# A new start, and one mixing product per unit on GpSimd, in a fused RWKV time-mixing kernel

## The chip, the cores and the metric

The kernel runs on one core of a Trainium2 chip. The metric is the device time of one execution in microseconds. The kernel before takes 228.21 us (median of three runs, 228.16 to 228.28). Five engines work side by side: TensorE (PE in the profile), VectorE (DVE), ScalarE (ACT), GpSimd (POOL) and SyncE (SP, which here only issues transfers). "L152" in a profile line is a line of the kernel whose profile it is; the two kernels have different line numbers.

## The reference, cut to what matters

`x` has the shape (16, 2048, 256), float32. Only two of the three mixed inputs reach the output:

```python
x_prev[:, 1:, :] = x[:, :-1, :]                    # row before, zero at the start
xv = x * time_mix_v + x_prev * (1 - time_mix_v)
xr = x * time_mix_r + x_prev * (1 - time_mix_r)
v = xv @ value_weight
r = xr @ receptance_weight
out = ((1 / (1 + np.exp(-r))) * v) @ output_weight  # float32
```

## The kernel before

The work is cut into 64 *units* of 512 rows, four to each of the 16 batches. A unit is: eight transposes of x on PE into PSUM, a copy of them to `xt` on ACT, a mixed input `mix` on DVE, two projections r and v on PE (eight matmuls of 512 columns), a sigmoid on ACT, the product `z` on DVE, the output projection on PE (eight matmuls of 256 columns), and a copy of it to SBUF on ACT. The mix factor is folded into the weights, so that mixing is a product of `xt` with a per-row constant and a sum with the next column block. Column slot 0 of `xt` is a copy of the last slot, shifted by one (the "wrap copy", once a batch).

```python
def mixing_scale(b, m, lo, hi):          # two products, ko = 0 and 1
    for ko in range(KO):
        nc.vector.tensor_scalar(out=mix[b][:, m, ko, lo:hi], in0=xt[b][:, ko, lo:hi],
            scalar1=c_sb[:, m, ko : ko + 1], scalar2=None, op0=ALU.mult)

def mixing_add(b, m, lo, hi):            # one sum
    nc.vector.tensor_tensor(out=mix[b][:, m, :, lo:hi], in0=mix[b][:, m, :, lo:hi],
        in1=xt[b][:, :, lo + P : hi + P], op=ALU.add)

for g in range(NU):                      # NU = 64
    ps_r = project(g, 0, ...)            # PE
    nc.scalar.activation(out=s_sb, in_=ps_r, func=ACT.Sigmoid)
    ps_v = project(g, 1, ...)            # PE
    # (cut: unit 0)
    took = take_pieces(g + 3, 1 if g > 8 else 2)
    for piece in took: mixing_scale(*piece)
    nc.vector.tensor_tensor(out=z_sb, in0=s_sb, in1=ps_v, op=ALU.mult)
    for piece in took: mixing_add(*piece)
    advance(START_T[g] if g < len(START_T) else g + LOOK)   # transposes of later units
    if z_prev is not None: output(g - 1, z_prev)
    z_prev = z_sb
```

A *piece* is half a batch (1024 columns) for one of the two inputs; in the steady stage one piece is mixed per unit, some units ahead. All PSUM accumulators have one buffer, those of the transposes two.

## Time and profile before

| | before |
|---|---|
| time, median | 228.21 us |
| profiled execution: time, span | 229.34, 227.6 us |
| DVE, PE, ACT, POOL busy | 203.4, 201.8, 185.4, 13.8 us |
| four units (one batch), middle | 12.57 us |
| start of z in units 0, 1, 2, 3, 5, 7 | 15.35, 19.12, 25.45, 30.63, 40.14, 46.26 us |

The busy shares, the chain, the groups and a unit's timeline are shown in the prediction below. What it only tells of is the start, so here it is: the timeline of the kernel before, columns start, duration, engine, line, operation, and in brackets how long the engine had stood idle and for what.

```profile
11.42 1.24 POOL L118 CAST wo_bf<-wo_f 128x512 bf16<-128x512 f32 x1 [7.38 <-DMA wo_f<-in_output_weight_dram]
...
12.61 1.15 POOL L72 DMA_DIRECT2D x_bf<-in_x_dram  x2
...
20.44 0.62 PE L128 MATMUL ps_t<-ident,x_bf 128*128 128x128 bf16 x8 [2.94 <-DMA x_bf<-in_x_dram]
```

GpSimd took the two in program order: it waited 7.38 us for the output weight before a cast, and only after that issued the load of batch 1, whose transposes therefore started at 20.44.

### The profile page before, as it was taken

What the parts mean: (1) busy time and instruction counts of PE and PEld (TensorE: products, weight loads), DVE (VectorE), ACT (ScalarE), POOL (GpSimd) and SP (SyncE); (2) the same over time, 40 slices, a digit from 0 to 9 for tenths busy, and PEclk for the clock granted to TensorE, in tenths of its full rate; (3) what the DMA queues carried; (4) which work ended last, traced back from release to release, by engine and by line L of the source; (5) the groups of instructions that cost most, each with busy time, mean ns of one, the idle gap of its engine ahead of it and who ended that gap; (6) DMA issues with size and microseconds to landing.
All of it is one profiled execution on the core that took longest, in us unless ns stands there. A gap on an engine that the chain in (4) does not pass through costs nothing.

```text
span 227.6 us, 3894 instructions
## 1 busy us (share of the span) xinstructions
PE 201.8 (89%) x1510; PEld 129.8 (57%) x1538; DVE 203.4 (89%) x288; ACT 185.4 (81%) x194; POOL 13.8 (6%) x41
## 2 busy tenths in 40 slices
PE   0294879899999999999999999999999999989881
PEld 0253547566666666665666566666666665655551
DVE  2478299999999999999999999999999999999941
ACT  2185789898989989899989899898989899985671
POOL 5050101000000101010000001010100000000000
PEclk9998899999999999999999999999999999999998
DMA  5969999999999898989999898989897444434364
GB/s 90 217 109 213 215 161 266 229 324 179 351 173 343 164 301 213 251 265 209 327 189 348 160 328 181 279 229 252 268 216 310 187 184 186 187 161 170 148 261 186
DMA packets 9155, 51.38 MB, mean 226 GB/s; under 512 B 1456, under 2 KB 2352, under 8 KB 3376
## 3 DMA queue, kind: packets, MB, share of 16 engines
q0 software_dynamic: 2736, 16.78, 43.9%
q1 hardware_dynamic: 6400, 34.35, 36.9%
q8 instruction: 12, 0.20, 0.3%
q14 instruction: 7, 0.06, 0.1%
HBM read 34.34 MB, written 33.55 MB: 298 GB/s over the span
## 4 chain that ended last, share of the span: by engine, by line
DVE 73%; issue 12%; PE 6%; DMA 3%; POOL 2%; ACT 2%; POOLq 0%; DVEq 0%
DVE mix L161 29%; DVE z_sb L295 29%; DVE mix L152 14%; DMA x_bf<-in_x_dram 3%; PE psum_o L192 2%; PE psum_v L176 2%; PE psum_r L176 1%; ACT xt L134 1%; DVE xt L136 1%; POOL x_bf L80 1%; POOL xt L124 1%; POOL wo_bf L118 1%; PE ps_t L128 0%; ACT o_sb L210 0%; DVE o_sb L207 0%
## 5 line engine op out<-in xcount | busy, mean ns | idle before, releaser
L176 PEld LDWEIGHTS <-w_bf 128*128 128x128 bf16 x512 | 50.3, 99 | 58.3 <-issue 12.4
L295 DVE TENSOR_TENSOR z_sb<-s_sb,psum_v 128x1024 bf16<-128x1024 bf16 x64 | 77.7, 1213 | 5.8 <-ACT s_sb L284 2.9
L161 DVE TENSOR_TENSOR mix<-mix,xt 128x2048 bf16<-128x2048 bf16 (+1 forms) x66 | 77.8, 1186 | 0.0
L134 ACT COPY xt<-ps_t 128x1024 bf16<-128x1024 bf16 x60 | 60.4, 1013 | 19.0 <-PE ps_t L128 18.9
L210 ACT COPY o_sb<-psum_o 128x1024 f32<-128x1024 f32 x63 | 64.2, 1019 | 6.9 <-PE psum_o L192 6.8
L176 PE MATMUL psum_v<-mix,w_bf 128*128 128x512 bf16 x243 | 64.9, 383 | 5.3 <-DVE z_sb L295 4.5
L284 ACT ACTIVATE s_sb<-psum_r 128x1024 bf16<-128x1024 f32 x64 | 66.6, 1041 | 1.4 <-PE psum_r L176 1.4
L192 PE MATMUL psum_o<-wo_bf,z_sb 128*128 128x256 bf16 x512 | 66.6, 273 | 1.1 <-ACT o_sb L210 1.1
L176 PE MATMUL psum_r<-mix,w_bf 128*128 128x512 bf16 x241 | 65.4, 388 | 1.6 <-DVE mix L161 1.2
L152 DVE TENSOR_SCALAR mix<-xt,c_sb 128x1024 bf16<-128x1024 bf16 (+1 forms) x132 | 56.4, 473 | 3.5 <-ACT xt L238 1.8
L192 PEld LDWEIGHTS <-z_sb 128*128 128x128 bf16 x512 | 47.8, 98 | 7.3 <-DVE z_sb L295 1.0
L128 PEld LDWEIGHTS <-x_bf 128*128 128x128 bf16 x480 | 31.4, 98 | 17.2 <-DMA x_bf<-in_x_dram 3.2
L128 PE MATMUL ps_t<-ident,x_bf 128*128 128x128 bf16 x480 | 36.1, 219 | 3.9 <-DMA x_bf<-in_x_dram 2.9
L72 POOL DMA_DIRECT2D x_bf<-in_x_dram x16 | 8.7, 544 | 121.6 <-PE ps_t L128 118.2
L238 ACT COPY xt<-ps_t 128x1024 bf16<-128x1024 bf16 x4 | 4.0, 1014 | 9.2 <-PE ps_t L232 9.2
L232 PE MATMUL ps_t<-ident,x_bf 128*128 128x128 bf16 x32 | 3.1, 265 | 5.7 <-DMA x_bf<-in_x_dram 5.7
L232 PEld LDWEIGHTS <-x_bf 128*128 128x128 bf16 x32 | 2.5, 119 | 6.6 <-DMA x_bf<-in_x_dram 6.2
L136 DVE COPY xt<-xt 128x254 bf16<-128x254 bf16 x15 | 3.3, 220 | 2.0 <-ACT xt L134 2.0
L111 DVE TENSOR_SCALAR w_bf<-w_f,tms 128x256 bf16<-128x256 f32 x4 | 1.2, 351 | 4.1 <-DMA w_f<-in_value_weight_dram 3.5
L124 POOL MEMSET xt<- 128x2 bf16 x15 | 1.7, 111 | 47.1 <-DVE xt L136 47.1
L145 PE MATMUL ps_t<-ident,x_bf 128*128 128x128 bf16 x2 | 0.4, 298 | 3.8 <-DMA x_bf<-in_x_dram 3.8
L100 DVE TENSOR_SCALAR tms<-tm_sb 128x4 f32<-128x4 f32 x1 | 0.2, 169 | 3.5 <-DMA tm_sb<-in_time_mix_v_dram 3.5
(18 smaller groups left out, 8.6 us busy)
## 6 DMA issues: line engine op xcount, KB each, us to landing
out_dram<-o_sb SPq DMA_DIRECT2D x30, 1024.0 KB, 6.5
x_bf<-in_x_dram POOLq DMA_DIRECT2D x15, 1024.0 KB, 10.2
out_dram<-o_sb SPq DMA_DIRECT2D x3, 512.0 KB, 2.8
x_bf<-in_x_dram POOLq DMA_DIRECT2D x2, 256.0 KB, 6.7
out_dram<-o_sb SPq DMA_DIRECT2D x2, 256.0 KB, 2.1
x_bf<-in_x_dram POOLq DMA_DIRECT2D x1, 448.0 KB, 9.4
w_f<-n_receptance_weight_dram SPq DMA_DIRECT2D x1, 256.0 KB, 3.0
w_f<-in_value_weight_dram SPq DMA_DIRECT2D x1, 256.0 KB, 6.6
```

The lines of the kernel that those rows point to most:

```text
L72: nc.gpsimd.dma_start(out=x_bf[b][:, lo:hi, :], in_=src[:, lo:hi, :])
L128: nc.tensor.transpose(out=ps[:, ko, jj * P : (jj + 1) * P], in_=x_bf[b][:, e * UJ + jj, ko * P : (ko + 1) * P], identity=ident,)
L134: nc.scalar.copy(out=xt[b][:, :, c0 : c0 + TU], in_=ps)
L136: nc.vector.tensor_copy(out=xt[b][:, :, 1:P], in_=xt[b][:, :, J * P : (J + 1) * P - 1])
L152: nc.vector.tensor_scalar(out=mix[b][:, m, ko, lo:hi], in0=xt[b][:, ko, lo:hi], scalar1=c_sb[:, m, ko : ko + 1], scalar2=None, op0=ALU.mult,)
L161: nc.vector.tensor_tensor(out=mix[b][:, m, :, lo:hi], in0=mix[b][:, m, :, lo:hi], in1=xt[b][:, :, lo + P : hi + P], op=ALU.add,)
L176: nc.tensor.matmul(out=ps[:, mo, :], lhsT=w_bf[:, m, ko, mo * P : (mo + 1) * P], rhs=mix[b][:, m, ko, e * TU : (e + 1) * TU], start=(ko == 0),
L192: nc.tensor.matmul(out=ps[:, jj, :], lhsT=z[:, ko, jj * P : (jj + 1) * P], rhs=wo_bf[:, ko, :], start=(ko == 0), stop=(ko == KO - 1),)
L210: nc.scalar.copy(out=o_sb[b][:, j0 : j0 + UJ, :], in_=ps)
L232: nc.tensor.transpose(out=ps[:, ko, jj * P : (jj + 1) * P], in_=x_bf[0][:, g * UJ + jj, ko * P : (ko + 1) * P], identity=ident,)
L284: nc.scalar.activation(out=s_sb, in_=ps_r, func=ACT.Sigmoid)
L295: nc.vector.tensor_tensor(out=z_sb, in0=s_sb, in1=ps_v, op=ALU.mult)
```

## The change

Its intent is to fill the pipeline sooner and to take one of DVE's two products per unit away, onto the idle GpSimd. The core of the diff, with cuts:

```diff
-    LOOK = 7
+    LOOK = 8
+    WARM = 34
+    WARM2 = 10
-    xtpool = ... bufs=2
+    xtpool = ... bufs=3
# start: the first unit and the last rows in float32, from SyncE; all of batches 0 and 1
# issued before any GpSimd arithmetic; weights scaled on GpSimd
+    nc.sync.dma_start(out=x_last, in_=rows(0)[:, J - 1, :])
+    nc.sync.dma_start(out=x_unit, in_=rows(0)[:, 0:UJ, :])
+    nc.scalar.dma_start(out=tm_sb[:, 0, :], ...)   # also tm_sb[:, 1, :]
+    nc.sync.dma_start(out=w_f32[:, 0], ...)
+    nc.scalar.dma_start(out=w_f32[:, 1], ...)
+    load(0, UJ, 2 * UJ)
+    load(0, 2 * UJ, J)
+    load(1)
+    for _ in range(WARM):
+        nc.tensor.matmul(out=warm[:, 0, 0:P], lhsT=zeros, rhs=zeros, start=True, stop=True)
-            nc.vector.tensor_scalar(out=w_bf[:, m, ko, :], ..., scalar2=None, op0=ALU.mult)
+            nc.gpsimd.tensor_scalar(out=w_bf[:, m, ko, :], ..., scalar2=1.0, op0=ALU.mult, op1=ALU.mult)
# ... (cut)
+    def scale_pool(piece, after):
+        op = nc.gpsimd.tensor_scalar(out=mix[b][:, m, 1, lo:hi], in0=xt[b][:, 1, lo:hi],
+            scalar1=c_sb[:, m, 1:2], scalar2=1.0, op0=ALU.mult, op1=ALU.mult)
+        if after is not None:
+            tc.add_manual_dep(op.ins, after.ins.name, SYNC, reason="one at a time")
# ... the loop, steady stage (START_POOL = 8)
+            for i in todo:
+                last = scale(pieces[i], (0,) if i in on_pool else (0, 1))
+        advance(START_T[g] if g < len(START_T) else g + LOOK)   # now ahead of v
         ps_v = project(g, 1, ps_v_pool, "psum_v")
         nc.vector.tensor_tensor(out=z_sb, in0=s_sb, in1=ps_v, op=ALU.mult)
+        if g >= START_POOL - 1 and done < len(pieces):
+            scale_pool(pieces[done], last)        # next unit's piece, ko = 1
+        for i in todo:
+            add(pieces[i])
+        wrap_slots()                              # the wrap copy, now a unit before its first reader
```

Batch 0 is mixed in pieces of one unit, later batches in halves; look-ahead of the mixing is eight pieces.

More of the change, by code (lines that the diff above doesn't have):

```diff
@@ L47 @@
     NU = B * UB
-    LOOK = 7
+    HALF = J * P // 2
+    LOOK = 8
+    WARM = 34
+    WARM2 = 10
     consts = ctx.enter_context(tc.tile_pool(name="consts", bufs=1))
     xpool = ctx.enter_context(tc.tile_pool(name="xpool", bufs=3))
-    xtpool = ctx.enter_context(tc.tile_pool(name="xtpool", bufs=2))
+    xtpool = ctx.enter_context(tc.tile_pool(name="xtpool", bufs=3))
     mixpool = ctx.enter_context(tc.tile_pool(name="mixpool", bufs=2))
@@ L61 @@
     ctx.enter_context(tc.manual_schedule())
+    SYNC = mybir.DependencyInfo(mybir.DependencyClass.Sync, mybir.DependencyReason.DATA)
     x_bf = {}
@@ L66 @@
     o_sb = {}
-    def load(b, pieces):
-        x_bf[b] = xpool.tile([P, J, D], BF16, name="x_bf")
-        src = x[b].rearrange("(p j) d -> p j d", p=P)
-        for lo, hi in pieces:
-            nc.gpsimd.dma_start(out=x_bf[b][:, lo:hi, :], in_=src[:, lo:hi, :])
-    ident = consts.tile([P, P], BF16)
-    load(0, [(J - 1, J)])
-    src0 = x[0].rearrange("(p j) d -> p j d", p=P)
-    def load0(lo, hi):
-        nc.gpsimd.dma_start(out=x_bf[0][:, lo:hi, :], in_=src0[:, lo:hi, :])
-    load0(0, 4)
@@ L83, with rows, load @@
-    make_identity(nc, ident)
-    load0(4, 8)
-    load0(8, 15)
+    zeros = consts.tile([P, P], BF16)
+    nc.vector.memset(zeros, 0.0)
+    ident_f = consts.tile([P, P], FP32)
+    make_identity(nc, ident_f)
+    ident = consts.tile([P, P], BF16)
+    nc.vector.tensor_copy(out=ident, in_=ident_f)
+    def rows(b):
+        return x[b].rearrange("(p j) d -> p j d", p=P)
+    def load(b, lo=0, hi=J):
+        if b not in x_bf:
+            x_bf[b] = xpool.tile([P, J, D], BF16, name="x_bf")
+        nc.gpsimd.dma_start(out=x_bf[b][:, lo:hi, :], in_=rows(b)[:, lo:hi, :])
@@ L87 @@
+    x_last = consts.tile([P, D], FP32)
+    x_unit = consts.tile([P, UJ, D], FP32)
     tm_sb = consts.tile([P, 2, KO], FP32)
     w_f32 = consts.tile([P, 2, KO, D], FP32)
-    for m, (tm, w) in enumerate(
-        [(time_mix_r, receptance_weight), (time_mix_v, value_weight)]
-    ):
-        nc.sync.dma_start(out=tm_sb[:, m, :], in_=tm.rearrange("(ko p) -> p ko", p=P))
-    for m, w in enumerate([receptance_weight, value_weight]):
-        nc.sync.dma_start(out=w_f32[:, m], in_=w.rearrange("(ko p) n -> p ko n", p=P))
@@ L95 @@
-    wo_f32 = consts.tile([P, KO, D], FP32)
-    nc.sync.dma_start(out=wo_f32, in_=output_weight.rearrange("(ko p) n -> p ko n", p=P))
+    wo_f32 = consts.tile([P, KO, D], FP32)
+    nc.sync.dma_start(out=x_last, in_=rows(0)[:, J - 1, :])
+    nc.sync.dma_start(out=x_unit, in_=rows(0)[:, 0:UJ, :])
+    nc.scalar.dma_start(out=tm_sb[:, 0, :], in_=time_mix_r.rearrange("(ko p) -> p ko", p=P))
+    nc.scalar.dma_start(out=tm_sb[:, 1, :], in_=time_mix_v.rearrange("(ko p) -> p ko", p=P))
+    nc.sync.dma_start(
+        out=w_f32[:, 0], in_=receptance_weight.rearrange("(ko p) n -> p ko n", p=P)
+    )
@@ new lines @@
+    nc.scalar.dma_start(
+        out=w_f32[:, 1], in_=value_weight.rearrange("(ko p) n -> p ko n", p=P)
+    )
+    nc.sync.dma_start(out=wo_f32, in_=output_weight.rearrange("(ko p) n -> p ko n", p=P))
+    sig0 = consts.tile([P, 1], BF16)
+    nc.scalar.activation(out=sig0, in_=zeros[:, 0:1], func=ACT.Sigmoid)
+    load(0, UJ, 2 * UJ)
+    load(0, 2 * UJ, J)
+    load(1)
+    warm = ps_o_pool.tile([P, UJ, D], FP32, name="psum_o")
+    for _ in range(WARM):
+        nc.tensor.matmul(out=warm[:, 0, 0:P], lhsT=zeros, rhs=zeros, start=True, stop=True)
@@ L98, with new_xt @@
+    def new_xt(b):
+        xt[b] = xtpool.tile([P, KO, (J + 1) * P], BF16, name="xt")
+        (nc.vector if b == 0 else nc.gpsimd).memset(xt[b][:, :, 0:1], 0.0)
+    new_xt(0)
     tms = consts.tile([P, 2, KO], FP32)
@@ L110 @@
         for ko in range(KO):
-            nc.vector.tensor_scalar(
+            nc.gpsimd.tensor_scalar(
                 out=w_bf[:, m, ko, :],
@@ L114 @@
                 scalar1=tms[:, m, ko : ko + 1],
-                scalar2=None,
+                scalar2=1.0,
                 op0=ALU.mult,
+                op1=ALU.mult,
             )
-    nc.gpsimd.tensor_copy(out=wo_bf, in_=wo_f32)
+    nc.gpsimd.tensor_scalar(
+        out=wo_bf, in0=wo_f32, scalar1=1.0, scalar2=1.0, op0=ALU.mult, op1=ALU.mult
+    )
     def transposes(g):
@@ L122, in transposes @@
         if e == 0:
-            xt[b] = xtpool.tile([P, KO, (J + 1) * P], BF16, name="xt")
-            nc.gpsimd.memset(xt[b][:, :, 0:1], 0.0)
+            new_xt(b)
         ps = ps_t_pool.tile([P, KO, TU], BF16, name="ps_t")
@@ L134, in transposes, with first_transposes, scale_act, scale @@
         nc.scalar.copy(out=xt[b][:, :, c0 : c0 + TU], in_=ps)
-        if e == UB - 1 and b > 0:
-            nc.vector.tensor_copy(
-                out=xt[b][:, :, 1:P], in_=xt[b][:, :, J * P : (J + 1) * P - 1]
-            )
-    def first_prev():
-        xt[0] = xtpool.tile([P, KO, (J + 1) * P], BF16, name="xt")
-        nc.vector.memset(xt[0][:, :, 0:1], 0.0)
-        ps = ps_t_pool.tile([P, KO, TU], BF16, name="ps_t")
+        if e == UB - 1:
+            late_copies.append(b)
+    def first_transposes():
+        pl = ps_v_pool.tile([P, KO, TU], FP32, name="psum_v")
         for ko in range(KO):
             nc.tensor.transpose(
-                out=ps[:, ko, 0:P], in_=x_bf[0][:, J - 1, ko * P : (ko + 1) * P], identity=ident
+                out=pl[:, ko, 0:P], in_=x_last[:, ko * P : (ko + 1) * P], identity=ident_f
             )
-        nc.vector.tensor_copy(out=xt[0][:, :, 1:P], in_=ps[:, :, 0 : P - 1])
-    def mixing_scale(b, m, lo, hi):
+        ps = ps_r_pool.tile([P, KO, TU], FP32, name="psum_r")
         for ko in range(KO):
-            nc.vector.tensor_scalar(
+            for jj in range(UJ):
+                nc.tensor.transpose(
+                    out=ps[:, ko, jj * P : (jj + 1) * P],
+                    in_=x_unit[:, jj, ko * P : (ko + 1) * P],
+                    identity=ident_f,
+                )
+        nc.vector.tensor_copy(out=xt[0][:, :, 1:P], in_=pl[:, :, 0 : P - 1])
+        nc.scalar.copy(out=xt[0][:, 0, P : P + TU], in_=ps[:, 0, :])
+        nc.vector.tensor_copy(out=xt[0][:, 1, P : P + TU], in_=ps[:, 1, :])
+    def scale_act(piece):
+        b, m, lo, hi = piece
+        for ko in range(KO):
+            nc.scalar.mul(
+                out=mix[b][:, m, ko, lo:hi], in_=xt[b][:, ko, lo:hi], mul=c_sb[:, m, ko : ko + 1]
+            )
+    def scale(piece, kos=(0, 1)):
+        b, m, lo, hi = piece
+        for ko in kos:
+            last = nc.vector.tensor_scalar(
                 out=mix[b][:, m, ko, lo:hi],
@@ L158, in mixing_scale, with add @@
             )
-    def mixing_add(b, m, lo, hi):
+        return last
+    def scale_pool(piece, after):
+        b, m, lo, hi = piece
+        op = nc.gpsimd.tensor_scalar(
+            out=mix[b][:, m, 1, lo:hi],
+            in0=xt[b][:, 1, lo:hi],
+            scalar1=c_sb[:, m, 1:2],
+            scalar2=1.0,
+            op0=ALU.mult,
+            op1=ALU.mult,
+        )
+        if after is not None:
+            tc.add_manual_dep(op.ins, after.ins.name, SYNC, reason="one at a time")
+    def add(piece):
+        b, m, lo, hi = piece
         nc.vector.tensor_tensor(
@@ L166, in mixing_add @@
         )
-    def new_mix(b):
-        mix[b] = mixpool.tile([P, 2, KO, J * P], BF16, name="mix")
     def project(g, m, pool, name):
@@ L215, in output, with needs, tile_for, per_unit @@
             nc.sync.dma_start(out=dst[:, a : a + 2 * UJ, :], in_=o_sb[b][:, a : a + 2 * UJ, :])
-    def t_unit(g):
-        b, e = divmod(g, UB)
-        if e == 0 and b + 1 < B and b + 1 not in x_bf:
-            load(b + 1, [(0, J)])
-        if g == 0:
-            return
-        transposes(g)
-    load(1, [(0, J)])
-    first_prev()
-    def transposes0(g):
-        ps = ps_t_pool.tile([P, KO, TU], BF16, name="ps_t")
-        for jj in range(UJ):
-            for ko in range(KO):
-                nc.tensor.transpose(
-                    out=ps[:, ko, jj * P : (jj + 1) * P],
-                    in_=x_bf[0][:, g * UJ + jj, ko * P : (ko + 1) * P],
-                    identity=ident,
-                )
-        c0 = (1 + g * UJ) * P
-        nc.scalar.copy(out=xt[0][:, :, c0 : c0 + TU], in_=ps)
-    tnext = 0
+    pieces = [
+        (0, m, u * TU, (u + 1) * TU) for u in range(UB) for m in range(2)
+    ] + [
+        (b, m, q * HALF, (q + 1) * HALF) for b in range(1, B) for q in range(2) for m in range(2)
+    ]
+    def needs(piece):
+        b, m, lo, hi = piece
+        return hi // TU - 1 if b == 0 else UB * b + UB - 1
+    def tile_for(piece):
+        if piece[0] not in mix:
+            mix[piece[0]] = mixpool.tile([P, 2, KO, J * P], BF16, name="mix")
+    def per_unit(g):
+        if g < len(START_MIX):
+            return START_MIX[g]
+        return min(len(pieces), g + 8)
+    START_T = [3, 5, 7, 9, 11]
+    START_MIX = [4, 6, 8, 10, 12]
+    START_POOL = 8
+    late_copies = []
+    def wrap_slots():
+        while late_copies:
+            b = late_copies.pop()
+            if b > 0:
+                nc.vector.tensor_copy(
+                    out=xt[b][:, :, 1:P], in_=xt[b][:, :, J * P : (J + 1) * P - 1]
+                )
+    tnext = 1
     def advance(limit):
@@ L245, in advance @@
             b, e = divmod(tnext, UB)
-            if e == 0 and b + 2 < B:
-                load(b + 2, [(0, J)])
-            if b == 0:
-                transposes0(tnext)
-            else:
-                transposes(tnext)
-            tnext += 1
-    HALF = J * P // 2
-    START_T = [3, 4, 7, 9]
-    pieces = [(h, m) for h in range(2 * B) for m in range(2)]
-    pnext = 2
-    def take_pieces(limit, most):
-        nonlocal pnext
-        took = []
-        while len(took) < most and pnext <= min(limit, len(pieces) - 1):
-            h, m = pieces[pnext]
-            b, q = divmod(h, 2)
-            if tnext <= UB * b + UB - 1:
-                break
-            if b not in mix:
-                mix[b] = mixpool.tile([P, 2, KO, J * P], BF16, name="mix")
-            took.append((b, m, q * HALF, (q + 1) * HALF))
-            pnext += 1
-        return took
-    advance(1)
-    mix[0] = mixpool.tile([P, 2, KO, J * P], BF16, name="mix")
-    for m in range(2):
-        mixing_scale(0, m, 0, TU)
-    for m in range(2):
-        mixing_add(0, m, 0, TU)
+            if e == 1 and b + 2 < B:
+                load(b + 2)
+            transposes(tnext)
+            tnext += 1
+    first_transposes()
+    for piece in pieces[0:2]:
+        tile_for(piece)
+    scale(pieces[0])
+    scale_act(pieces[1])
+    add(pieces[0])
+    add(pieces[1])
+    advance(1)
+    for _ in range(WARM2):
+        nc.tensor.matmul(out=warm[:, 0, 0:P], lhsT=zeros, rhs=zeros, start=True, stop=True)
+    done = 2
+    on_pool = set()
     z_prev = None
     for g in range(NU):
+        todo = list(range(done, per_unit(g)))
+        for i in todo:
+            assert needs(pieces[i]) < tnext, (g, i)
+            tile_for(pieces[i])
+        done = max(done, per_unit(g))
         ps_r = project(g, 0, ps_r_pool, "psum_r")
@@ L284 @@
         nc.scalar.activation(out=s_sb, in_=ps_r, func=ACT.Sigmoid)
-        ps_v = project(g, 1, ps_v_pool, "psum_v")
-        if g == 0:
-            for m in range(2):
-                mixing_scale(0, m, TU, 2 * TU)
-            for m in range(2):
-                mixing_add(0, m, TU, 2 * TU)
-        took = take_pieces(g + 3, 1 if g > 8 else 2)
-        for piece in took:
-            mixing_scale(*piece)
+        last = None
+        if g == 0:
+            for i in todo:
+                scale(pieces[i])
+            for i in todo:
+                add(pieces[i])
+            todo = []
+        elif g < START_POOL:
+            for i in todo[:-1]:
+                scale(pieces[i])
+                add(pieces[i])
+            if todo:
+                last = scale(pieces[todo[-1]])
+        else:
+            for i in todo:
+                last = scale(pieces[i], (0,) if i in on_pool else (0, 1))
+        advance(START_T[g] if g < len(START_T) else g + LOOK)
+        ps_v = project(g, 1, ps_v_pool, "psum_v")
         z_sb = zpool.tile([P, KO, TU], BF16, name="z_sb")
         nc.vector.tensor_tensor(out=z_sb, in0=s_sb, in1=ps_v, op=ALU.mult)
-        for piece in took:
-            mixing_add(*piece)
-        advance(START_T[g] if g < len(START_T) else g + LOOK)
+        if late_copies and done < len(pieces) and pieces[done][0] in late_copies:
+            wrap_slots()
+        if g >= START_POOL - 1 and done < len(pieces):
+            tile_for(pieces[done])
+            assert needs(pieces[done]) < tnext
+            scale_pool(pieces[done], last)
+            on_pool.add(done)
+        if g < START_POOL:
+            todo = todo[-1:]
+        for i in todo:
+            add(pieces[i])
+        wrap_slots()
         if z_prev is not None:
```

## The prediction

> **What bounds the kernel now.** I read first the busy shares, then the chain that ended last, then the groups of instructions, then the timeline of one unit in the middle and of the last units.
>
> ```profile
> PE 201.8 (89%) x1510; PEld 129.8 (57%) x1538; DVE 203.4 (89%) x288; ACT 185.4 (81%) x194; POOL 13.8 (6%) x41
> ...
> DVE 73%; issue 12%; PE 6%; DMA 3%; POOL 2%; ACT 2%; POOLq 0%; DVEq 0%
> ```
>
> Two engines show the same 89%, so busy time doesn't choose between them. The chain does: 73% of the span is DVE, 6% PE. GpSimd (POOL) is idle.
>
> ```profile
> L295 DVE TENSOR_TENSOR z_sb<-s_sb,psum_v 128x1024 bf16<-128x1024 bf16 x64 | 77.7, 1213 | 5.8 <-ACT s_sb L284 2.9
> L161 DVE TENSOR_TENSOR mix<-mix,xt 128x2048 bf16<-128x2048 bf16 (+1 forms) x66 | 77.8, 1186 | 0.0
> ...
> L152 DVE TENSOR_SCALAR mix<-xt,c_sb 128x1024 bf16<-128x1024 bf16 (+1 forms) x132 | 56.4, 473 | 3.5 <-ACT xt L238 1.8
> ```
>
> These three groups are DVE's work in a unit (512 rows): z, one sum, two products. Durations overlap a little at their ends, so I work with start-to-start times ("pitch"), from the timeline of a unit in the middle:
>
> ```profile
> 123.79 0.61 PE L128 MATMUL ps_t<-ident,x_bf 128*128 128x128 bf16 x8
> 123.93 0.88 DVE L152 TENSOR_SCALAR mix<-xt,c_sb 128x1024 bf16<-128x1024 bf16 x2
> ...
> 124.24 1.04 PE L192 MATMUL psum_o<-wo_bf,z_sb 128*128 128x256 bf16 x8
> ...
> 124.72 1.21 DVE L295 TENSOR_TENSOR z_sb<-s_sb,psum_v 128x1024 bf16<-128x1024 bf16 x1
> ...
> 125.85 1.22 DVE L161 TENSOR_TENSOR mix<-mix,xt 128x2048 bf16<-128x2048 bf16 x1
> ...
> 126.99 0.22 DVE L136 COPY xt<-xt 128x254 bf16<-128x254 bf16 x1
> ```
>
> DVE: two products 0.79 (123.93 to 124.72), z 1.13, sum 1.14: 3.06 us. Once per batch of four units a wrap copy adds 0.33 (0.22 plus a short wait). A batch takes 4 x 3.06 + 0.33 = 12.57 us, as the chain has it (its products start at 64.88, 77.45, 90.01), or 3.14 per unit. ACT's three instructions have a pitch of about 0.9 each, some 2.75.
>
> PE is the engine to look at next. In the last units there are no transposes, and PE alone sets the pace:
>
> ```profile
> 215.69 0.81 PE L176 MATMUL psum_r<-mix,w_bf 128*128 128x512 bf16 x3
> ...
> 216.55 1.03 PE L176 MATMUL psum_v<-mix,w_bf 128*128 128x512 bf16 x4
> ...
> 217.41 1.04 PE L192 MATMUL psum_o<-wo_bf,z_sb 128*128 128x256 bf16 x8
> ...
> 218.28 1.03 PE L176 MATMUL psum_r<-mix,w_bf 128*128 128x512 bf16 x4
> ```
>
> From 215.69 to 218.28 is 2.59 us for the two projections and the output. The eight transposes add 0.45 (123.79 to 124.24 above): **3.04 us per unit is what PE needs**, only 0.10 under today's 3.14.
>
> **What the Trainium skill says.** (1) "TensorE: Matmul & The Clock Gate", section "Wait — 56ns, not 53.3ns?": warm matmuls start N / 2.4 GHz + 2.5 ns apart, 55.6 ns for 128 columns, 215.7 for 512. Eight of each, with eight of 256 columns at 109 ns, make 3.04 us: the trace agrees. So 3.04 is a floor, not a schedule. (2) "SBUF — State Buffer", section "Who interferes with whom": a DVE instruction in a two-port mode, or with two SBUF inputs while GpSimd reads SBUF, shares a port with GpSimd, and the second to start waits; one with at most one SBUF input in neither mode doesn't contend. The mixing products and sums are of the first two kinds. z (one input in PSUM) is of the last, which is why the GpSimd product is held until DVE's own product is done. Before has one possible case: the GpSimd cast of the output weight took 1.24 us for 512 elements while DVE ran two sums; I can't tell from it alone. (3) "GPSIMD Engine Reference", section "3.1 Elementwise — side-by-side cycle accounting": 1.03 to 1.8 cycles per element at 1.2 GHz for a simple one-input body. For 1024 elements that is an estimate of 0.9 to 1.55 us plus dispatch. No row of before has this instruction.
>
> **The change, part by part.**
>
> (a) *Steady stage.* From unit 7 on, 53 of the 120 large products move to GpSimd. DVE per unit: 0.40 + 1.13 + 1.14 = 2.67 us; per batch 4 x 2.67 + 0.33 = 11.0, or 2.75. DVE falls below PE. Only 0.10 of the 0.39 saved per unit reaches the time, since PE takes over at 3.04. The reordering on PE (transposes before the v projection, output last) leaves the cycle feasible: from one v to the next, z (1.2 with its wait) must end before PE has done an output, an r and eight transposes (2.2). PE should hardly wait. Over about 48 units with transposes that is 48 x 0.10 = 4.8 us. The tail of 7.1 us after the last z stays.
>
> GpSimd: product start to its end must fit beside DVE's wait for z and z itself. If it holds the sum back fully, the DVE loop is its duration D + sum 1.14 + product 0.40 + about 0.1 for signals, so D up to 1.4 is free. I take D = 1.1.
>
> (b) *Fill.* Before, the first r projection starts at 11.7, but the worse loss is later: batch 1's load was issued only at 12.6, behind a GpSimd cast that waited for the output weight, and landed at 20.4. The DMA engines were only 0.67 busy from 11.4 to 17.1. z number 0, 1, 2, 3, 4, 5 and 7 start at 15.4, 19.1, 25.5, 30.6, 35.6, 40.1 and 46.3: up to 6 us per unit. After, all loads of batch 0 and 1 are issued ahead of any GpSimd arithmetic, by about 3.5 us. From 17.1 to 22.8 the queue brought 217 GB/s counted in bf16, so twice that in float32. The 4.9 MB ahead (0.63 + 0.75 + 1.5 + 2.0) at some 0.4 MB per us, plus 2 to 3 us, put batch 1 at about 15.5.
>
> My walk through the start (estimates from the pitches above; product of 512 columns 0.285, its sum 0.61, first unit's data at about 6.2, since one 0.5 MB piece needed 5.5 us before): float32 transposes until 8, mixing on DVE and ACT side by side until 10.2, r(0) there, warm. z(0) 13.6. z(1) waits for batch 1 and v: 17.3. From there DVE sets the pace: units 2, 3 and 4 carry two pieces each (3.5, 4.8 and 5.3 us, the last two with four full products and two full sums), units 5 to 7 one each. z(2) 21, z(3) 25.8, z(4) 31.1, z(5) 34.3, z(7) 40.5. Against 46.3 that is 5.8 us. DVE then outruns PE and recovers about 0.8 us by z(10).
>
> (c) *Small things.* Weight scaling goes to GpSimd while DVE waits for x anyway; the sigmoid table is loaded early, which saves 1.28 us of ACT ahead of s(0) but is part of the walk. The extra float32 load of the last rows is 0.13 MB. The two warm-up groups use idle PE time.
>
> *Sum.* z(10) at 48.8, 45 units at 3.04 = 136.8, eight without transposes at 2.6 = 20.8, so the last z at 206.4 and the end at 213.5. The time is 0.6 above the span (228.2 against 227.6): 214.1. I add 0.9 for a few PE waits and say **215.0 us**, a gain of 13.2: about 5 from the steady stage and the rest from the fill.
>
> **The rivals.**
>
> *GpSimd is slower than thought.* If D is 1.55 and the sum waits for all of it, a unit costs 3.19 and the steady gain vanishes: about 221. At D = 2.3 it is 3.94, and 56 units lose 45 us. For it: the 1.24 us cast, and the upper figure of the skill. Against it: that cast collided with DVE sums, and this product is placed where DVE does z.
>
> *DMA becomes the bound.* A batch reads and writes 4.19 MB; in the window 52.31 to 64.88 of before the DMA share was 0.93. At 12.16 us per batch it would be 0.96. For it: so little room. Against it: loads run about seven units ahead, land in 10.2 us, and the output has three buffers, so latency may grow unseen. If it binds, the batch costs perhaps 12.4 us and the time is about 218.
>
> *The fill gains nothing.* Batch 1 still lands near 20 because the weights and the float32 unit share the engines, and PE now stalls in front of v(1). Then z(1) is at about 22, some 4 to 5 us of the gain are lost: 219 to 220.
>
> *Better than said:* DVE's start is limited by arithmetic I counted in full; if ACT or the loads are earlier, 211 is possible.
>
> **Range and chances.** Main line 215; the three mild rivals each put it at 218 to 221; the good case 211. Eight in ten: 210.5 to 221. A gain over 2% needs under 223.6: it survives each mild rival alone. Only a slow GpSimd, or two rivals together, prevents it. Faster 0.90, within 2% 0.06, slower 0.04.
>
> **What would show it.** In the middle, a batch of four units should take 12.2 us with PE's idle time near none and the chain on PE; DVE should be busy about 180 us. The GpSimd product should have a mean of 0.9 to 1.4 us, and the sum's mean stay near 1.2: a longer sum or z means a blocked port. Batch 1's transposes should start near 16 and z(7) near 40. It is wrong if products on GpSimd last over 1.5 us, if DVE still leads the chain in the steady stage, or if PE waits on x there.

## The result, and the profile after

The changed kernel takes **219.25 us** (median of four runs, 218.68 to 220.65), the kernel before in the same rounds 228.19. A ratio is the mean time of one kernel's fast runs over that of the other's of the same rounds, so not quite the ratio of these medians: 0.9617, with a 95% interval of 0.9571 to 0.9663. These runs, and all that have a state below, are in the fast state.

| | before | after |
|---|---|---|
| profiled execution: time, span | 229.34, 227.6 | 219.04, 217.3 |
| DVE, PE, ACT, POOL busy | 203.4, 201.8, 185.4, 13.8 | 186.5, 203.5, 184.4, 73.9 |
| four units, middle | 12.57 | 12.19 |
| z of unit 0, 1, 2, 3, 5, 7 starts | 15.35, 19.12, 25.45, 30.63, 40.14, 46.26 | 15.64, 19.52, 23.04, 27.96, 36.27, 42.39 |
| last z starts | 220.46 | 209.45 |

First the page of the changed kernel: its busy line, the chain by engine, and three groups (busy time and mean duration in ns, then idle time of the engine ahead of them).

```profile
PE 203.5 (94%) x1554; PEld 135.2 (62%) x1582; DVE 186.5 (86%) x238; ACT 184.4 (85%) x196; POOL 73.9 (34%) x96
...
PE 82%; ACT 6%; DMA 5%; issue 3%; DVE 1%; POOL 1%; ACTq 0%
...
L200 POOL TENSOR_SCALAR mix<-xt,c_sb 128x1024 bf16<-128x1024 bf16 x53 | 59.1, 1115 | 104.1 <-DVE mix L189 91.0
L355 DVE TENSOR_TENSOR z_sb<-s_sb,psum_v 128x1024 bf16<-128x1024 bf16 x64 | 78.0, 1219 | 17.2 <-PE psum_v L225 13.2
L213 DVE TENSOR_TENSOR mix<-mix,xt 128x2048 bf16<-128x2048 bf16 (+1 forms) x68 | 79.3, 1168 | 0.2
```

The chain has gone over from DVE (73% to 1%) to PE (6% to 82%). The new GpSimd product takes 1.115 us. z keeps its mean (1.213 before); the group of sums mixes two sizes, and the large ones alone go from 1.218 to 1.226, so next to nothing of it is paid by DVE. z now stands waiting for v from PE, 13.2 us in all.

The timeline of one unit in the middle, as for the kernel before:

```profile
120.77 1.11 POOL L200 TENSOR_SCALAR mix<-xt,c_sb 128x1024 bf16<-128x1024 bf16 x1 [1.19 <-DVE mix L189]
120.95 1.22 DVE L355 TENSOR_TENSOR z_sb<-s_sb,psum_v 128x1024 bf16<-128x1024 bf16 x1 [0.29 <-PE psum_v L225]
...
122.08 1.22 DVE L213 TENSOR_TENSOR mix<-mix,xt 128x2048 bf16<-128x2048 bf16 x1
...
123.22 0.48 DVE L189 TENSOR_SCALAR mix<-xt,c_sb 128x1024 bf16<-128x1024 bf16 x1
...
124.00 1.22 DVE L355 TENSOR_TENSOR z_sb<-s_sb,psum_v 128x1024 bf16<-128x1024 bf16 x1 [0.29 <-PE psum_v L225]
```

From z to z is 3.05 us. The GpSimd product lies from 120.77 to 121.88. It starts in the 0.29 us in which DVE waits for v, runs beside z (120.95 to 122.17), and is over before the sum starts at 122.08.

Last, the start of the changed kernel, again from the timeline:

```profile
12.63 2.03 POOL L132 TENSOR_SCALAR w_bf<-w_f,tms 128x256 bf16<-128x256 f32 x2 [2.50 <-DMA w_f<-in_value_weight_dram]
...
14.26 1.27 PE L225 MATMUL psum_v<-mix,w_bf 128*128 128x512 bf16 x4 [0.30 <-POOL w_bf L132]
...
15.64 1.22 DVE L355 TENSOR_TENSOR z_sb<-s_sb,psum_v 128x1024 bf16<-128x1024 bf16 x1 [1.78 <-PE psum_v L225]
...
17.35 0.62 POOL L140 TENSOR_SCALAR wo_bf<-wo_f 128x512 bf16<-128x512 f32 x1 [2.70 <-DMA wo_f<-in_output_weight_dram]
...
17.48 1.07 PE L151 MATMUL ps_t<-ident,x_bf 128*128 128x128 bf16 x16 [1.09 <-ACT s_sb L335]
17.91 0.58 POOL L86 DMA_DIRECT2D x_bf<-in_x_dram  x1
```

z(0) isn't earlier than before (15.64 against 15.35). The value weight landed at 12.54 and its scaling held v(0) until 14.26, but PE stood only 0.30 us for it. Batch 1's transposes start 3 us earlier than before, at 17.48, and that is where the start gains: 2.4 of the 3.9 us are there at z(2). The other 1.5 come between z(2) and z(5), where DVE in the kernel before waits 2.03 us for batch 1's copy to `xt`.

One thing that the traces show is needed for the runs on the start below. In the changed kernel PE has batch 1's transposes ahead of v(1) in its order. The load of batch 1 landed at 17.44 here. In all nine traces with this order (this one, and runs 1, 3, 4, 5, 6, 9, 10 and 11) z(1) starts 2.08 or 2.09 us after that landing, which moves from 16.60 to 17.58, while z(0) moves from 14.63 to 16.04 without any effect on z(1). So the landing of batch 1 sets the start from z(1) on, and not z(0).

The old fault is still there, one batch on: the load of batch 2 is issued at 17.91, behind a GpSimd instruction that waited for the output weight. It costs little: z(3) comes 4.92 us after z(2), against 4.71 in the runs where batch 2 landed sooner (9 and 11).

### The profile page after: what moved, and what is told of

Read it like the earlier page. It is cut to its first block, busy times and chain, and to the rows that moved or that the text cites. A ratio compares the mean times of both kernels' runs of the same rounds, so it can differ in the third digit from the quotient of the medians.

```text
span 217.3 us, 4050 instructions
## 1 busy us (share of the span) xinstructions
PE 203.5 (94%) x1554; PEld 135.2 (62%) x1582; DVE 186.5 (86%) x238; ACT 184.4 (85%) x196; POOL 73.9 (34%) x96
## 4 chain that ended last, share of the span: by engine, by line
PE 82%; ACT 6%; DMA 5%; issue 3%; DVE 1%; POOL 1%; ACTq 0%
PE psum_o L241 26%; PE psum_v L225 24%; PE psum_r L225 22%; PE ps_t L151 11%; DMA w_f<-in_value_weight_dram 5%; ACT s_sb L335 3%; ACT o_sb L259 1%; POOL w_bf L132 1%; ACT xt L157 1%; DVE z_sb L355 1%; DVE mix L189 0%; DVE o_sb L256 0%; ACT o_sb L254 0%; ACTq L96 0%; ACTq L95 0%
## 5 line engine op out<-in xcount | busy, mean ns | idle before, releaser
L200 POOL TENSOR_SCALAR mix<-xt,c_sb 128x1024 bf16<-128x1024 bf16 x53 | 59.1, 1115 | 104.1 <-DVE mix L189 91.0
L355 DVE TENSOR_TENSOR z_sb<-s_sb,psum_v 128x1024 bf16<-128x1024 bf16 x64 | 78.0, 1219 | 17.2 <-PE psum_v L225 13.2
L213 DVE TENSOR_TENSOR mix<-mix,xt 128x2048 bf16<-128x2048 bf16 (+1 forms) x68 | 79.3, 1168 | 0.2
L225 PEld LDWEIGHTS <-w_bf 128*128 128x128 bf16 x512 | 47.7, 98 | 36.4 <-issue 2.4
L241 PEld LDWEIGHTS <-z_sb 128*128 128x128 bf16 x512 | 50.1, 98 | 20.5 <-DVE z_sb L355 1.0
L151 PEld LDWEIGHTS <-x_bf 128*128 128x128 bf16 x504 | 33.1, 99 | 17.4 <-DMA x_bf<-in_x_dram 4.6
L151 PE MATMUL ps_t<-ident,x_bf 128*128 128x128 bf16 x504 | 38.0, 221 | 3.2 <-ACT s_sb L335 2.4
L189 DVE TENSOR_SCALAR mix<-xt,c_sb 128x1024 bf16<-128x1024 bf16 (+1 forms) x81 | 35.9, 458 | 0.0
L86 POOL DMA_DIRECT2D x_bf<-in_x_dram x17 | 9.9, 585 | 8.5 <-PE ps_t L151 8.4
L132 POOL TENSOR_SCALAR w_bf<-w_f,tms 128x256 bf16<-128x256 f32 x4 | 3.1, 775 | 8.4 <-DMA w_f<-n_receptance_weight_dram 5.9
L112 PE MATMUL psum_o<-zeros 128*128 128x128 bf16 x34 | 3.8, 313 | 1.0 <-DVE zeros L74 1.0
L112 PEld LDWEIGHTS <-zeros 128*128 128x128 bf16 x34 | 3.5, 149 | 1.0 <-DVE zeros L74 1.0
## 6 DMA issues: line engine op xcount, KB each, us to landing
x_bf<-in_x_dram POOLq DMA_DIRECT2D x15, 1024.0 KB, 12.1
```

What stands on the lines that cost most here:

```text
L86: nc.gpsimd.dma_start(out=x_bf[b][:, lo:hi, :], in_=rows(b)[:, lo:hi, :])
L112: nc.tensor.matmul(out=warm[:, 0, 0:P], lhsT=zeros, rhs=zeros, start=True, stop=True)
L151: nc.tensor.transpose(out=ps[:, ko, jj * P : (jj + 1) * P], in_=x_bf[b][:, e * UJ + jj, ko * P : (ko + 1) * P], identity=ident,)
L189: last = nc.vector.tensor_scalar(out=mix[b][:, m, ko, lo:hi], in0=xt[b][:, ko, lo:hi], scalar1=c_sb[:, m, ko : ko + 1], scalar2=None, op0= ...
L200: op = nc.gpsimd.tensor_scalar(out=mix[b][:, m, 1, lo:hi], in0=xt[b][:, 1, lo:hi], scalar1=c_sb[:, m, 1:2], scalar2=1.0, op0=ALU.mult, op1 ...
L225: nc.tensor.matmul(out=ps[:, mo, :], lhsT=w_bf[:, m, ko, mo * P : (mo + 1) * P], rhs=mix[b][:, m, ko, e * TU : (e + 1) * TU], start=(ko == 0),
```

## The experiments

Twelve runs in three sets, each set on one chip with the kernel before beside it. The kernel before wasn't equally steady everywhere: in the first set its runs went from 227.95 to 230.65. Small differences of times are therefore read inside one set, and ratios of different sets aren't compared to the last per cent: the changed kernel itself has 0.9617 in its first measurement and 0.9541 in the last set.

**1. Without the GpSimd product.** The theory: the gain is two sums, one of the start and one of the steady stage. Rivals: one of them gives all.

```diff
-    START_POOL = 8
+    START_POOL = 99
```

> The changed kernel with its new fill kept and all mixing products on the Vector engine again. Theory (the gain is two separate sums: the fill about 3 to 4 us up to z(7), the GpSimd product about 7 us from z(7) to the last z): the Vector engine goes back to 3.06 us per unit and 12.57 per batch of four units, the time is about 225, some 1.5% under the kernel before. Rival 1 (the fill alone gives the gain): about 219 to 220. Rival 2 (the GpSimd product alone gives it): about 228.

Measured: 223.81 us (223.65 to 224.33), ratio 0.9761 (0.9704 to 0.9817). Both rivals fall: the start and the new order are worth 2.4% without GpSimd. The chain is DVE's again, and around the wrap copy the timeline reads:

```profile
DVE 73%; DMA 9%; issue 8%; PE 7%; ACT 1%; POOL 1%; ACTq 0%; POOLq 0%; DVEq 0%
```

```profile
131.31 0.23 DVE L297 COPY xt<-xt 128x254 bf16<-128x254 bf16 x1
131.44 0.89 DVE L189 TENSOR_SCALAR mix<-xt,c_sb 128x1024 bf16<-128x1024 bf16 x2
```

z(7) starts at 42.46, as in the changed kernel. But a batch takes 12.37 us, not the 12.57 that I expected: in the new order the instruction after the wrap copy belongs to an earlier batch and doesn't read what the copy wrote, so the copy adds 131.44 - 131.31 = 0.13 us and not 0.33 (before, the copy started at 126.99 and the product that reads it at 127.31). The new order gives half of the gain per batch by itself.

**2. The old start with the GpSimd product.** The same question from the other side: the kernel before with the held product (from unit 9 on), look-ahead 8, three `xt` buffers.

```diff
-    LOOK = 7
+    LOOK = 8
-    xtpool = ... bufs=2
+    xtpool = ... bufs=3
+        if g >= 9 and pnext < len(pieces):     # next piece's ko = 1, after z
+            scale_pool(*nxt, last)
```

> The kernel before with its old fill, and only the GpSimd product added (from unit 9 on, held back in the same way, look-ahead 8 and three xt buffers as that needs). Theory (two separate sums): a batch takes 12.2 us and the time is 221 to 222.5. Rival 1 (the fill gives the gain): about 228. Rival 2 (the product gives all of it): 219. If the placing of the transposes in the PE order matters for the product to pay, the batch stays over 12.4 us.

Measured: 222.91 us (221.94 to 224.07), ratio 0.9717 (0.9657 to 0.9777), a batch 12.2 us, and PE leads the chain with 83%. So the product pays in the old PE order too. The two parts overlap. Counted in the traces by the start of the last z, run 1 is 6.4 us ahead of the kernel before, run 2 7.3, the changed kernel 11.0. The missing 2.7 us are nearly what the new place of the wrap copy gives in run 1 (13 batches of 0.20): both parts shorten DVE's batch, and PE's floor takes what goes beyond 12.2.

**3. Without the hold.** GpSimd's product waits for its data only.

```diff
-            scale_pool(pieces[done], last)
+            scale_pool(pieces[done], None)
```

> The changed kernel without the extra wait that holds the GpSimd product back until the unit's own Vector product is done; all data waits stay. Port theory: GpSimd products now meet Vector sums and products, so their mean goes from 1.12 to 1.3 us or more and the mean of the 2048-column sum or the product rises by 0.1 us or more; with 0.3 us of Vector slack per unit the time is 219 to 223. Rival (no shared port, the hold does nothing): all means unchanged, time the same within 0.5 us.

Measured: 226.10 us (225.66 to 226.25), ratio 0.985 (0.9803 to 0.9898). The direction is the port theory's, the size is over what it named. The timeline shows why (GpSimd and DVE of one batch):

```profile
109.59 4.05 POOL L200 TENSOR_SCALAR mix<-xt,c_sb 128x1024 bf16<-128x1024 bf16 x3
...
110.22 1.34 DVE L189 TENSOR_SCALAR mix<-xt,c_sb 128x1024 bf16<-128x1024 bf16 x1
...
111.49 1.20 DVE L355 TENSOR_TENSOR z_sb<-s_sb,psum_v 128x1024 bf16<-128x1024 bf16 x1
...
112.62 2.10 DVE L213 TENSOR_TENSOR mix<-mix,xt 128x2048 bf16<-128x2048 bf16 x1
```

Unheld, GpSimd runs the products of a whole batch in a burst as soon as the `mix` buffer comes free. The DVE product grows from 0.48 to 1.34 us, the sum from 1.22 to 2.10; only z, with one input in PSUM, keeps 1.20. The mean of the large sums goes from 1.226 to 1.401 us, of the large DVE products to 0.644. DVE is busy 204.8 us again, as before the change. So one line of waiting is worth some 5 to 7 us: 5.3 by the ratios (0.985 against 0.9617, of two sets), 6.9 by the medians.

**4. Is PE the bound?** Half of the output matmuls left out, a wrong result.

```diff
-            for ko in range(KO):
+            for ko in range(1):        # start=True, stop=True
                 nc.tensor.matmul(out=ps[:, jj, :], lhsT=z[:, ko, ...], rhs=wo_bf[:, ko, :], ...)
```

> The changed kernel with half of the output matmuls left out, wrong on purpose: PE needs 2.61 us per unit in place of 3.04. If PE is the bound, the pace falls to that of the next engine (Vector 2.75, Scalar about 2.77 us per unit, so 11.1 us per batch) and the time to 205 to 208. If the DMA is next at what it can bring, about 11.6 to 11.9 us per batch and 211 to 214. If PE isn't the bound (Vector still is), the time stays at 217 to 219.

Measured: 206.22 us (205.53 to 206.97). PE was the bound. A batch takes 11.05 us (z at 66.36 and 77.41), and DVE leads the chain:

```profile
DVE 54%; issue 29%; DMA 7%; PE 5%; another core or an unknown queue 1%; POOL 1%; ACT 1%; DVEq 0%; POOLq 0%
```

DVE and ACT are both busy for the whole of that batch. From 60 to 180 us no engine waits for a transfer, so the DMA has not bound even at that pace, which clears the second rival of the prediction.

**5. Held until z is done**, so that the product starts beside the sum: the port by itself.

```diff
+        z_op = nc.vector.tensor_tensor(out=z_sb, ...)
-            scale_pool(pieces[done], last)
+            scale_pool(pieces[done], z_op)
```

> The changed kernel with the GpSimd product held until z is done, so that it starts beside the sum. Port theory (the two-input sum and the GpSimd read exclude one another): the sum (1.22 us) or the GpSimd product (1.12 us) of each unit grows by up to 1 us; if one waits out the other in full, a unit takes about 1.13 + 1.1 + 1.14 + 0.4 = 3.8 us and the time about 255 to 265; if they share, about 3.3 us and 230 to 240. Rival (no port conflict): sum and product keep their means, the Vector engine keeps 2.67 us per unit, and the time stays at 219 to 220.

Measured: 245.93 us (one run; the lengths below are from its trace), between the two sizes named. Its timeline:

```profile
102.39 1.21 DVE L213 TENSOR_TENSOR mix<-mix,xt 128x2048 bf16<-128x2048 bf16 x1
...
102.63 1.95 POOL L200 TENSOR_SCALAR mix<-xt,c_sb 128x1024 bf16<-128x1024 bf16 x1 [1.25 <-DVE z_sb L355]
...
103.53 1.34 DVE L189 TENSOR_SCALAR mix<-xt,c_sb 128x1024 bf16<-128x1024 bf16 x1
```

The sum started first and keeps 1.21 us. The GpSimd product takes 1.95: it ends 0.98 us after the sum does, a little less than its own 1.115. The DVE product, which comes third, takes 1.34 and ends 0.29 us after the GpSimd one, less than its own 0.48. In this trace the first holds each time and the next waits. A unit then takes 3.53 us (z at 101.26 and 104.79), 0.86 more than DVE's 2.67: not one whole GpSimd product is added, as I had it. By these lengths a part of each waiting instruction passes while it waits.

**6. One multiplication in place of two.** The changed kernel multiplies by the constant and again by 1.0. Is that only a quicker path?

```diff
-            scalar2=1.0, op0=ALU.mult, op1=ALU.mult,
+            scalar2=None, op0=ALU.mult,
```

> The changed kernel with the GpSimd product written as a single multiplication, without the second multiplication by 1.0. Theory A (the second operation only selects a quicker path): the product gets longer than 1.12 us, 1.5 us or more, and the time rises by 1 us or more once it passes about 1.4 us. Theory B (one operation less is at least as quick): 0.9 to 1.12 us, and the time stays at 219 to 220, since PE is the bound.

Measured: 235.71 us (235.62 to 236.33), ratio 1.0327: slower than the kernel before.

```profile
L200 POOL TENSOR_SCALAR mix<-xt,c_sb 128x1024 bf16<-128x1024 bf16 x53 | 150.8, 2845 | 30.6 <-DVE mix L189 18.8
```

```profile
L200 POOL TENSOR_SCALAR mix<-xt,c_sb x53: 2842/2843/2850, 42.2 to 215.2; 128x1024 bf16<-128x1024 bf16 x53
```

The single multiplication takes 2.85 us where the double one takes 1.115. It outlasts z and lies beside sum and product, and the large DVE product grows to 0.894. The second line, from the view of line 200, gives the least, the median and the longest of the 53 in ns: they agree within 8 ns, though the sums beside them take anything from 1.23 to 1.45 us. In every one GpSimd starts before the sum does. So the 2.85 us is the instruction's own time, as far as a trace can tell, and the waiting is DVE's.

**7. Big loads later.** The start's theory: the value weight, which lands at 12.6 behind the big loads, sets z(0).

```diff
     load(0, UJ, 2 * UJ)
-    load(0, 2 * UJ, J)
-    load(1)
     # between the scaling of the first and of the second weight:
+    load(0, 2 * UJ, J); load(1); load(2)
-    START_T = [3, 5, 7, 9, 11]
+    START_T = [3, 3, 7, 9, 11]
```

> The changed kernel with the big loads (rows 8 to 15 of batch 0, batch 1, batch 2) issued behind the first weight's scaling on GpSimd, batch 2 no longer behind the output weight, and batch 1's transposes moved one unit later. Theory (the value weight, landing at 12.6 behind the big loads, sets z(0)): it lands by 9, z(0) starts near 14 in place of 15.6, z(2) near 21 in place of 23.0, and the time is about 217. Rival (the total of bytes sets the start, not their order): z(2) stays within 0.5 us of 23 and the time at 219 or more.

Measured: 224.02 us (222.69 to 224.89), a miss. The weight did land sooner (7.9 us after its issue, against 10.8), but I had moved the wait: rows 8 to 15 of batch 0 were issued at 11 and landed at 16.2, and PE, which has their transposes ahead of v(0), stood:

```profile
16.25 1.89 PE L153 MATMUL ps_t<-ident,x_bf 128*128 128x128 bf16 x16 [3.95 <-DMA x_bf<-in_x_dram]
```

z(0) started at 19.95. Nor is that all: with `START_T` changed too, four units' transposes stand ahead of v(2), and z(2) waited 2.59 us for v. The steady stage was untouched (3.05 us per unit).

**8. The same with one piece less of look-ahead in the mixing.** I took the two large pieces in unit 4 for front-loaded work that could wait. `LOOK`, the look-ahead of the transposes, went down by one with it.

```diff
-    LOOK = 8
+    LOOK = 7
-    START_MIX = [4, 6, 8, 10, 12]
+    START_MIX = [4, 6, 8, 10]
-        return min(len(pieces), g + 8)
+        return min(len(pieces), g + 7)
```

> As the one before, and with one unit less of look-ahead in the mixing, so that only unit 3 carries two large pieces on the Vector engine and not units 3 and 4. Theory (from z(3) on the Vector engine's front-loaded work sets the start): z(4) comes about 3.3 us after z(3) in place of 5.1, and the time is 1 to 1.5 us under the one before, about 215.5 to 216. Rival (PE is what sets it there): within 0.4 us of the one before.

Measured: 238.75 us, ratio 1.0444, a clear miss. z(4) did come 3.56 us after z(3), but in every second unit of the steady stage v now waits for the sum of the unit just ahead. The table of waits (who for whom, total, times, longest):

```profile
PE psum_v L227 <- DVE mix L215: 13.2, 30, 1.1
```

The eighth piece of look-ahead isn't a luxury: in this trace a z starts at 111.21, the sum behind it ends at 113.57, 2.4 us later, and PE is ready for the next unit's v at 113.28, 2.1 us later.

**9 to 12. What the parts of the start are worth.** One set, five rounds, with the changed kernel itself as the yardstick (run 9); run 10 is without the warm-up, 11 has the first unit in bf16, 12 a mended order of the loads.

> The changed kernel itself, unchanged, timed beside the three others of this set as their yardstick: 219.0 to 219.6 us, as in its first measurement (218.7 to 220.7).

Measured: 218.65 us (218.41 to 218.73), ratio 0.9541 (0.9513 to 0.9568); the kernel before was at 229.25 (227.99 to 230.15) here.

No warm-up:

```diff
-    WARM = 34
+    WARM = 0
-    WARM2 = 10
+    WARM2 = 0
```

> The changed kernel without the 44 warm-up matmuls. Theory (z(0) hangs on the value weight, which lands at 12.6, and PE has slack before it): the first transposes and r(0) run at half speed, 1 to 2 us more of PE work, of which most hides; z(0) later by 0 to 1 us, time 219 to 220.5. Rival (warm PE is a main part of the fill's gain): 221 or more.

Measured: 219.17 us (218.58 to 221.10), ratio 0.9576 (0.9539 to 0.9614). In the trace r(0) takes 1.86 us for its four matmuls, which start 0.43 us apart, against 0.22 in run 9. But with the warm-up they don't always go faster: in the first profile of the changed kernel, and in the next run, some or all of r(0)'s matmuls are 0.43 us apart as well. By the medians the warm-up is worth half a microsecond, and the intervals overlap. z(0) comes 1.17 us later than in run 9 and z(1) 0.16 earlier, with batch 1's landing: the fill's gain isn't there.

First unit in bf16, through GpSimd's queue, as in the kernel before:

```diff
-    x_last = consts.tile([P, D], FP32)
+    x_last = consts.tile([P, D], BF16)
-    x_unit = consts.tile([P, UJ, D], FP32)
+    x_unit = consts.tile([P, UJ, D], BF16)
-    nc.sync.dma_start(out=x_last, ...)      # and x_unit
+    nc.gpsimd.dma_start(out=x_last, ...)    # and x_unit; transposes into ps_t, in bf16
```

> The changed kernel with the first unit and the last row block loaded in bf16 through GpSimd again and transposed in bf16, all else kept. Theory (the float32 unit isn't what sets z(0); the value weight is): z(0) within 0.7 us of 15.6 and the time within 1 us of the changed kernel. Rival (the float32 load is what starts the fill earlier): z(0) later by 1.5 us or more and the time 221 or more.

Measured: **217.31 us** (217.20 to 217.44), ratio 0.9484 (0.9457 to 0.9512), below the changed kernel's interval of the same set and the fastest of all: 217.31 / 218.65 is 0.6% less. The theory said "within 1 us"; it is 1.3 us faster. Its start:

```profile
5.97 1.83 POOL L132 TENSOR_SCALAR w_bf<-w_f,tms 128x256 bf16<-128x256 f32 x4 [1.70 <-DVE tms L124]
...
7.79 0.61 POOL L140 TENSOR_SCALAR wo_bf<-wo_f 128x512 bf16<-128x512 f32 x1
...
8.35 0.58 POOL L86 DMA_DIRECT2D x_bf<-in_x_dram  x1
```

Without 0.63 MB of float32 ahead of them the weights land 3.5 to 5.0 us after issue (5.4 to 13.7 in run 9). They are scaled by 7.8 in place of 13.9 in run 9, and batch 2's load goes out at 8.35 in place of 16.44. z(0) is at 15.29 all the same (14.87 in run 9): the first unit's data come later now. z(1) to z(7) are 0.7 us earlier (18.68 to 41.33 against 19.36 to 42.02), and so is the last z, 208.40 against 209.08. What carries this over is batch 1, which landed at 16.60 in place of 17.28; its transposes, first in run 9 and then here:

```profile
17.32 1.07 PE L151 MATMUL ps_t<-ident,x_bf 128*128 128x128 bf16 x16 [1.70 <-DMA x_bf<-in_x_dram]
```

```profile
16.64 1.07 PE L151 MATMUL ps_t<-ident,x_bf 128*128 128x128 bf16 x16 [0.59 <-DMA x_bf<-in_x_dram]
```

Whether it lands sooner for the bytes that are saved or for the new order of the queues, this run doesn't separate. The other 0.8 of the 1.5 us between the two spans isn't the start's at all: after the last output has landed, SyncE runs seven closing semaphore instructions in run 9 and one here, and the program ends 1.71 and 0.94 us after that landing.

A mended order of the loads, with the GpSimd product from unit 5 on:

```diff
     load(0, 2 * UJ, J)
-    load(1)
     # between the scaling of the first and of the second weight:
+    load(1); load(2)
-    START_POOL = 8
+    START_POOL = 5
     # in unit 1 the transposes come after v
```

> The changed kernel with the loads of batches 1 and 2 behind the first weight's scaling (rows 8 to 15 of batch 0 stay ahead, which the earlier try missed), unit 1's transposes behind its v projection, and the GpSimd product started three units earlier. Theory (value weight sets z(0), loads' order can be mended): value weight lands by 10.5, z(0) near 14, z(2) near 22, z(7) near 41, time 217 to 218. Rival (any order only moves the wait): z(2) at 23 or later and 219 or more.

Measured: 218.15 us (218.03 to 220.69), ratio 0.9527 (0.9494 to 0.9560): not to be told from the changed kernel. In the trace the value weight still took 10.6 us, batch 1's transposes started at 19.90 after 2.54 us of waiting for their data, and z(2) at 24.57: there the order only moved the wait, as the rival has it. But the profiled execution is the slowest of the seven (220.69 us), and its last z is 2.0 us later than in run 9. What the start looked like in the six others isn't known, three things were changed at once, and the rival's "219 or more" wasn't met. So run 12 leaves the rival open.

## Why the prediction was right

The time, 219.25, is inside the range of 210.5 to 221.0, in its upper part; the direction and the reason are as predicted, the point of 215.0 was 4 us low. By its steps:

- *PE's floor.* 3.04 us per unit and 12.2 per batch were predicted; 3.05 and 12.19 measured, with the chain on PE (82%), and run 4 shows by taking PE work away that it is the bound.
- *The GpSimd product.* D = 1.1 was chosen out of an estimate of 0.9 to 1.55, and 1.115 measured: that it fits so closely is luck. The large sum's mean did not grow (1.218 and 1.226). The first rival fell, though run 6 shows how near it was: the same product written with one multiplication lasts 2.85 us and ends at 235.71, slower than before. The rival's sum would give 4.5 us per unit at that D; 3.34 was measured, because the sums did not wait for all of it.
- *DMA as the bound.* Its share is 0.94 and 0.96 in two batches of the middle (60.02 and 108.76 on) with 0.96 foreseen, landings went from 10.2 to 12.1 us, and PE doesn't wait for x there. Run 4 went on to 11.05 us per batch.
- *The fill.* This is the term that was mis-sized. The closing split, about 5 us from the steady stage and 8 from the fill, isn't what the prediction's own figures give: they have 5.8 us by z(7) and 8.3 from there to the last z. Measured are 3.9 and 7.1. The step that failed is the landing of batch 1: put at about 15.5, it came at 17.44, with the transposes at 17.48 (16 foreseen) and z(1) at 19.52 (17.3 foreseen). From z(1) on, DVE's steps were right: z(2), z(3), z(4), z(5) and z(7) at 23.04, 27.96, 33.07, 36.27 and 42.39 are each about 2 us after the walk's figure, and run 11, where batch 1 lands 0.68 us earlier than in run 9, moves them all by as much. The bytes ahead were not the fault, by luck: rows 4 to 15 were counted as 0.75 and 1.5 MB where they are 0.5 and 1.0 in float32 (256 and 512 KB in bf16 on the page), and the weights' 0.8 MB were left out, so that 4.9 MB stand against 5.1. What was too fast was "0.4 MB per us, plus 2 to 3 us": 5.1 MB by 17.44, less 2.5 us, are about 0.34. The third rival, "the weights and the float32 unit share the engines" and PE stalls in front of v(1), came true in part, at 17.4 and not near 20.
- *z(0)* was 2.0 us late as well, 15.64 for 13.6: r(0) started at 11.15 and not at 10.2, its matmuls were up to 0.43 us apart where the walk has them warm, and v(0) then waited 0.30 us for the value weight. But it counts for nothing: in run 9 z(0) is at 14.87 and z(1) only 0.16 us earlier.
- *The end.* The eight units without transposes took 2.68 us each, not 2.6: DVE's 2.67 is the longer one there. That is 0.7 us. After the last z came 7.85 us, not 7.1: these are the closing semaphore instructions of run 11's account, seven here and one in the kernel before.
- *From span to time.* I added 0.6 us. The profiled execution of the kernel before was one of its slower ones: 229.34 for a span of 227.6. The difference is 1.74 there, and 219.04 - 217.3 = 1.74 in the changed kernel.

The account closes: start 2.1, steady stage 0.3, units without transposes 0.7, after the last z 0.75, span to time 1.15, less the 0.9 that I had added for waits, is 4.1 us; 215.0 + 4.1 is the 219.04 of the profiled run to within 0.1. One sign missed its size: DVE is busy 186.5 us, not about 180.

One thing the prediction had not seen at all: the new place of the wrap copy. Run 1 puts it at 0.20 us per batch, half of the gain per batch, and it comes without GpSimd.

What stays open: what mixing batch 0 unit by unit is worth by itself, which was not run, and why batch 1 came at 0.34 MB per us.

## What to carry to other kernels

When two engines are nearly even, work out the second one's floor from a stage in which it runs alone (here the last units) before counting what the first one saves: of 0.39 us taken from DVE per unit, only 0.10 reached the time. The product moved to GpSimd was free here beside z, and cost 7 us unheld (run 3) and 27 us beside the sum (run 5); the wait that put it beside z was worth more than half of the whole gain. In a start, find the one transfer that the later units hang on before mending others: look for a distance that stays the same from run to run (here 2.08 us from batch 1's landing to z(1)), and look at what an in-order engine waits for before it issues the next load.

## What the Trainium skill lacked or had wrong

- "SBUF — State Buffer", section "Who interferes with whom": agrees where it could be read. The second to start waits for the first: a DVE product went from 0.48 to 1.34 us, a sum from 1.22 to 2.10 behind a burst of GpSimd products, and a GpSimd product from 1.12 to 1.95 behind a sum, while z (one input in PSUM) kept 1.20. It doesn't fit run 6, where large sums under a running GpSimd product of the single form went only from 1.226 to 1.309 us, while the large DVE products did wait (0.48 to 0.89).
- "GPSIMD Engine Reference", section "3.1 Elementwise — side-by-side cycle accounting": its 1.03 to 1.8 cycles per element hold for the form with two operations (1.115 us for 1024 elements is 1.31 cycles at 1.2 GHz, dispatch included). It lacks that the same product written with one operation is the slow one: 2.85 us in run 6, which is an estimate of 3.3 cycles per element at the page's 1.2 GHz. The cast of the output weight points the same way, without being a test of it: 1.24 us for 512 elements before, 0.62 written with two multiplications.
- No page that I used says how long a transfer takes behind the others of a start: 256 KB of weights took 10.8 us in the changed kernel and 5.0 us without the float32 unit ahead, and the 2 MB of batch 1 took 14.8 and 12.9.
